# Up-projection in three token blocks with one-bank matmuls, and the weights' Winograd sums kept in DRAM

## The chip, the cores and the metric

One core of one Trainium2 chip. The metric is the device time of one execution in microseconds (us), the median of the runs shown; smaller is better.

## The reference, cut to what matters

One encoder layer in float32 on 2048 + 256 tokens of width 1024: an mLSTM group and a GQA group side by side, then a feed-forward part with a centred depthwise convolution of width 3 over the tokens. The change touches the feed-forward part:

```python
x = x + jnp.concatenate([m_out, a_out], axis=-1) @ w_out
h = rmsnorm(x, norm2_w)
u = centred_dwconv(h @ w_up, conv_w, conv_b)      # w_up: 1024 x 5632
a, g = jnp.split(u, 2, axis=-1)
return x + (jax.nn.silu(g) * a) @ w_down          # w_down: 2816 x 1024
```

Both request groups have the same weights, so the kernel treats the 2304 tokens as one axis and mends the convolution at the seam (token 2048).

## The kernel before, in words

Every product is made of float32r matmuls: an operand is split into a high part (a ScalarE copy) and a low part (a VectorE subtract of the copy from the source), and three matmuls high x high, high x low, low x high are accumulated in PSUM.

The stages follow one another: projections, attention and mLSTM side by side, the output projection with the second RMSNorm (`phase_c`, "C"), the up-projection (`phase_u`, "U") and the down-projection (`phase_e`, "E"). C writes the normalised activations to DRAM (`n2_d`).

**U.** The up-projection is a Winograd product of 2x2 blocks: seven products in place of eight. Tokens go in two blocks of `BLK` = 1152; `DT` gives the columns that each block computes, 1160 and 1144 (a few are shared with the next block's convolution and carried over in `carry`). Each block is cut into two token halves of 580 or 572 columns, and K = 1024 into two halves of four 128-row chunks. For a block, `n2_ops` holds seven activation operands in SBUF ("11", "21", "t2", "t1", "t3", "22", "t4"), each as high and low part of four chunks. The four "t" operands are sums that `n2_sums` makes beforehand on GpSimd (GpSimd DMAs in, four subtracts of 286 or 290 columns a half, DMAs out to `n2t_d`): for block 0 during C, for block 1 during groups 3 to 6 of block 0 (`SG`). `n2_load` reads an operand with two SyncE DMAs, two ScalarE copies and two VectorE subtracts (L1171, L1172).

The weights go in 22 "ups" a block (`up_start`), each for two output chunks of 128 columns, two ups (gate, then value) to a group. An up reads two raw weight tiles (L1206, SyncE, 512 KB each, a ring of two ups); GpSimd makes four weight sums of 512 columns (L1245 to L1248); for each of the seven products ScalarE makes the high part (L1233) and VectorE the low part (L1234), into a ring of five weight tiles (`WU`). `mul` then issues 24 matmuls (L1238): two token quarters of 290 or 286 columns, four chunks, three terms. So an up is 168 matmuls, and U is 44 ups of them. A PSUM tile is two banks, one for each quarter, and four such tiles take turns. ScalarE copies (L1256) and VectorE additions with one input in PSUM (L1259) combine the products to `u`.

The convolution follows for each chunk (`conv`): ScalarE writes the middle tap and the bias (L1341), VectorE adds the two outer taps (`scalar_tensor_tensor`, L1348, four an up). After the value up VectorE multiplies gate and value (L1367, one an up on average). GpSimd makes the four sums that E needs (L1371 to L1376) and stores seven operands to `a_d` (L1357).

**E.** It computes the down-projection in the same way, in seven passes with 384 columns a matmul (L1567). Its operands come by SyncE DMAs (`acts`: tiles `te`, 768 KB; `weight`: tiles `dw`, 256 KB), each split by ScalarE (L1409) and VectorE (L1410).

The order on each engine is written by a scheduler at build time from the program order and from priorities (`high_priority` raises them); on the chip every queue runs in that order. Memory of the pools is a stack: a pool that is opened takes the place of closed ones, and a tile's first write waits for the last reader of what lay there.

Of the kernel before, what the change touches and what calls it, by code (L numbers as in the profile page):

```python
# [17 lines left out]
P = 128  # L18
D = 1024
# [16 lines left out]
BLK = 1152  # L36
# [10 lines left out]
NH = 580  # L47
NW = 2 * NH + 1
DT = (0, 2 * NH, T)
HB = BLK // 2  # L50
TW = T // 2
N2A, N2B = 1280, 1024
# [33 lines left out]
P0 = ((V, V),) * 4  # L86
P1 = ((V, V),) * 7
LOP = ()
DLAG = 6
SEGS = ((0, NT1), (NT1, NT))  # L90


def f32(ap):
    return ap.bitcast(F32)
# [940 lines left out]
def phase_c(g, sn, sp, pp, wps):  # L1035
# [64 lines left out]
    def tail_b(b, x, ps, r):  # L1100
        r = rstd_rows(g, ps, r, BT)
        for z in range(NCC):
            nc.vector.scalar_tensor_tensor(x[:, z], x[:, z], g.n2w[:, z:z + 1], r, ALU.mult, ALU.mult)
            if z % 4 == 3:
                if b * BT < N2A:
                    g.st.dma_start(g.n2_d[0][:, z - 3:z + 1, b * BT:(b + 1) * BT], x[:, z - 3:z + 1])
                if b * BT >= N2B:
                    g.st.dma_start(g.n2_d[1][:, z - 3:z + 1, b * BT - N2B:(b + 1) * BT - N2B], x[:, z - 3:z + 1])
        g.normed.add(b)
# [10 lines left out]
    for n, b in enumerate(order):  # L1120
        x, mx = nxt
        for z in range(4):
            if z == 1 and n + 1 < NB:
                yield 2 * order[n + 1], C_MM
                nxt = loads(n + 1, order[n + 1])
            po = pp.tile([P, 2, BT], F32, tag="po", name=f"po{b}_{z}")
            for k, _ in enumerate(mm(b, z, mx, po)):
                if z == 1 and k == 0 and prev is not None:
                    tail_b(*prev)
                if z < 3 or k < 3:  # L1130
                    yield None, C_MM
            if z == 0:
                if prev is not None:
                    prev = (*prev[0:2], *tail_a(*prev))
                acc = sp.tile([P, 2, BT], F32, tag="acc", name=f"cacc{b}", bufs=1)
            post(b, z, x, po, acc)
            if (n, z) > (5, 0) and sums:

                n2_sums(g, sp, 0, sums.pop(0), tag="rn", bufs=2)
        prev = (b, x, acc)  # L1140
# [8 lines left out]
EARLY, LATE = OPS[:3], OPS[3:]  # L1149
# [7 lines left out]
def n2_load(g, ops, b, k, engs=("vector", "vector")):  # L1157


    nc = g.nc  # L1160
    n = (DT[b + 1] - DT[b]) // 2
    if k[0] == "t":
        i, h = SUMS[k]
        src = g.n2t_d[b, i, :, :, h]
    else:
        t = DT[b] - (0, N2B)[b] + n * (int(k[1]) - 1)
        src = g.n2_d[b][:, NCC // 2 * (int(k[0]) - 1):, t:t + n]
    for z in range(0, NCC // 2, 2):
        hi, lo = (ops[k][:, z:z + 2, a, 0:n] for a in range(2))
        nc.sync.dma_start(f32(lo), src[:, z:z + 2, 0:n])  # L1170
        nc.scalar.activation(hi, f32(lo), AF.Copy)  # L1171
        getattr(nc, engs[z // 2]).tensor_tensor(lo, f32(lo), f32(hi), ALU.subtract)  # L1172
# [6 lines left out]
def n2_sums(g, pool, b, c, engs=("gpsimd",) * 4, tag="tc", bufs=3):  # L1179


    nc = g.nc
    n = (DT[b + 1] - DT[b]) // 2
    m = n // 2
    for z in range(2):
        rs = []
        for k in range(2):
            r = pool.tile([P, NH], F32, tag=tag, name=f"rn{b}_{c}_{z}_{k}", bufs=bufs)[:, 0:n]
            r = r.rearrange("p (h t) -> p h t", h=2)
            src = g.n2_d[b][:, c + NCC // 2 * k, DT[b] - (0, N2B)[b]:DT[b + 1] - (0, N2B)[b]].rearrange("p (h t) -> p h t", h=2)  # L1190
            nc.gpsimd.dma_start(r, src[:, :, z * m:z * m + m])
            rs.append(r)
        (b11, b12), (b21, b22) = ((r[:, 0], r[:, 1]) for r in rs)
        for eng, (o, p, q) in zip(engs, ((b11, b12, b11), (b12, b22, b12), (b22, b22, b11), (b21, b21, b22))):
            getattr(nc, eng).tensor_tensor(o, p, q, ALU.subtract)
        for k in range(2):
            nc.gpsimd.dma_start(g.n2t_d[b, k, :, c, :, z * m:z * m + m], rs[k])
# [17 lines left out]

def up_start(g, s1, bank, ops, b, jj, rs=None):
# [4 lines left out]
    m = n // 2  # L1221
# [6 lines left out]
    def mul(p, k, src, add=False):  # L1228
# [6 lines left out]
        for z in range(2):  # L1235
            for c in range(NCC // 2):
                for i, (aa, bb) in enumerate(((0, 0), (0, 1), (1, 0))):
                    nc.tensor.matmul(p[:, z], w[:, aa, c, :], ops[k][:, c, bb, z * m:z * m + m],  # L1238
                                     start=c == 0 and i == 0 and not add, stop=c == NCC // 2 - 1 and i == 2,
                                     skip_group_check=add)  # L1240
    p1, p2 = bank("a" + nm)[:, :, 0:m], bank("b" + nm)[:, :, 0:m]
# [3 lines left out]
    nc.gpsimd.tensor_tensor(t1, a21, a22, ALU.add)  # L1245
    nc.gpsimd.tensor_tensor(t2, t1, a11, ALU.subtract)
    nc.gpsimd.tensor_tensor(a21, a11, a21, ALU.subtract)
    nc.gpsimd.tensor_tensor(t4, a12, t2, ALU.subtract)  # L1248

    def rest(u1, u2):  # L1250


        u11, u12, u21, u22 = (u[:, k * n:k * n + n].rearrange("p (z t) -> p z t", z=2) for u in (u1, u2) for k in range(2))
# [10 lines left out]
        p3 = bank("c" + nm)[:, :, 0:m]  # L1264
# [14 lines left out]
def phase_u(g, tc, s1, pd, ops, first):  # L1279
# [5 lines left out]
    with ExitStack() as st:  # L1285
        sa = st.enter_context(tc.tile_pool(name="d_a", bufs=1, reuse_waits="tile"))
        for k in range(YB):
            sa.tile([P, BLK], F32, tag="y", name=f"place_y{k}", bufs=YB)
        for k in range(3):
            sa.tile([P, NH], F32, tag="tc", name=f"place_tc{k}", bufs=3)  # L1290
# [18 lines left out]
        late.update(n2_ops(sl2, 0, ("t3", "t1")))  # L1309
        late = {k: late[k] for k in LATE}  # L1310
        for k, e in zip(LATE, P0):
            n2_load(g, late, 0, k, engs=e)
# [3 lines left out]
        def bank(nm):  # L1316
            return banks(g, pd[(g.nbank + 1) // 2 % 2], "p" + nm)
        for b in range(ND):
            nn = DT[b + 1] - DT[b]
            if b:  # L1320
                ops = n2_ops(s1[0], b, EARLY)
                ops.update(n2_ops(sl, b, ("t4", "22")))
                ops.update(n2_ops(sl2, b, ("t3", "t1")))
                for k, e in zip(OPS, P1):
                    n2_load(g, ops, b, k, engs=e)
# [33 lines left out]
            for gi, gr in enumerate(groups):  # L1359
                if b < ND - 1 and SG <= gi < SG + NCC // 2:  # L1360
                    n2_sums(g, sa, b + 1, gi - SG)
                ygs = up(gr[0] + NFC)
# [6 lines left out]
                t1, t2, t4 = (sa.tile([P, NH], F32, tag="tc", name=f"tc{k}_{b}_{gi}", bufs=3)[:, 0:HB] for k in (1, 2, 4))  # L1369
# [11 lines left out]
def phase_e(g, tc, pd):  # L1381
# [5 lines left out]
    with ExitStack() as st:  # L1387
        sx = st.enter_context(tc.tile_pool(name="e_t", bufs=1, reuse_waits="tile"))
        for k in range(TR):
            sx.tile([P, 2, TG, CG], F32R, tag="t", name=f"place_t{k}", bufs=TR)  # L1390
        swa = st.enter_context(tc.tile_pool(name="e_w", bufs=1, reuse_waits="tile"))
        for k in range(WRA):
            swa.tile([P, 2, h], F32R, tag="w", name=f"place_wa{k}", bufs=WRA)
        sr = st.enter_context(tc.tile_pool(name="e_r", bufs=1, reuse_waits="tile"))
        for k in range(DW):
            sr.tile([P, h], F32, tag="dw", name=f"place_dw{k}", bufs=DW)
        sc = st.enter_context(tc.tile_pool(name="e_c", bufs=1, reuse_waits="tile"))
        quad = {k: sc.tile([P, 4, TW], F32, name="c%d%d" % k) for k in ((0, 1), (0, 0), (1, 0), (1, 1))}
        sy = st.enter_context(tc.tile_pool(name="e_x", bufs=1, reuse_waits="tile"))
        for k in range(2):  # L1400
            sy.tile([P, 4, h], F32, tag="x", name=f"place_x{k}", bufs=2)
        sms = {(hf, z): sy.tile([P, CG], F32, tag=f"sm{hf}{z}", name=f"sm{hf}{z}") for hf in range(2) for z in range(G3)}
# [123 lines left out]
        fetch_w(WA)  # L1526
        fetch_t(2)
# [82 lines left out]
def body(tc, aps, phases="abcd"):  # L1610
# [5 lines left out]
    with ExitStack() as st:  # L1616
# [9 lines left out]
        g.n2_d = [dp.tile([P, NCC, n], F32, name=f"n2_d{k}") for k, n in enumerate((N2A, T - N2B))]  # L1626
# [3 lines left out]
        g.a_d = [dp.tile([7, P, min(TG, NP - p), TW], F32, name=f"a_d{p}") for p in range(0, NP, TG)]  # L1630
        g.s_d = [[dp.tile([P, D // 2], F32, name=f"s_d{k}_{p}") for p in range(NP)] for k in range(4)]
# [66 lines left out]
        pd = [pool(s5, "d_u", bufs=1, space=PSUM)]  # L1698
        g.nbank = -1
        with ExitStack() as s2:  # L1700
# [15 lines left out]
            first = [up_start(g, s1, lambda nm: banks(g, pd[(g.nbank + 1) // 2 % 2], "p" + nm), ops, 0, NFC, rs)]  # L1716
            g.c_end()
            s_wo.close()
            pd.append(pool(s5, "d_v", bufs=1, space=PSUM))
            phase_u(g, tc, s1, pd, ops, first)  # L1720
# [94 lines left out]
```

## Time and profile before

| | |
|---|---|
| median of 3 runs | 3371.27 us (3369.89 to 3371.71) |
| the profiled execution | 3363.86 us, its span 3361.9 us |
| mean granted TensorE clock | 0.990 |
| DVE busy | 2399.9 us, 71% |
| ACT busy | 1803.6 us, 54% |
| POOL busy | 1355.2 us, 40% |
| U's matmuls | from 1806.8 us to 2836.5 us |
| E's matmuls | from 2843.6 us on |

PE is TensorE, DVE VectorE, ACT ScalarE, POOL GpSimd, SP SyncE. In a table of windows each engine's busy time stands beside the number of instructions in brackets, then the granted clock, the share of time that the 16 DMA engines were busy, and GB/s. In a list of groups a line gives the source line, the engine, the operation, the tiles written and read, the shape and the count, then the busy time and the mean ns of one, then idle time before it. In a view of one source line, "a/b/c" are the least, the median and the longest duration in ns. In a list of waits a line names who waited, for whom, how long in total, how often, and the longest.

### The profile page before, as it was taken

The numbers are of one execution on the slowest core, as the hardware profiler recorded it, in microseconds if no ns is written. First come the engines' busy times: TensorE is split into PE (matmuls) and PEld (weight loads), VectorE is DVE, ScalarE is ACT, GpSimd is POOL, SyncE is SP. The second block draws the span as 40 slices with busy tenths as digits, with TensorE's granted clock in tenths as the row PEclk, the third lists the DMA queues.
The fourth block names the chain that finished last, engine by engine and source line by source line (L and its number), as shares of the span: only waits on it lengthen the run. The fifth ranks groups of instructions, "written<-read, shape, count | busy, mean of one in ns | idle before, by whom it ended". The sixth has DMA issues, their size and how long they took to land. (4 is left out here: it accounts for less than half of the span.)

```text
span 3361.9 us, 57158 instructions
## 1 busy us (share of the span) xinstructions
PE 3262.6 (97%) x21366; PEld 3038.9 (90%) x21366; DVE 2399.9 (71%) x3721; ACT 1803.6 (54%) x3799; POOL 1355.2 (40%) x1710
## 2 busy tenths in 40 slices
PE   8899999999999999899999999999999999999998
PEld 6788888888888888788888999999999998999998
DVE  7866687777768778976765778978877776453573
ACT  5546666667666777655553544446555555323331
POOL 8653033213333323421245457744544442751112
PEclk9999999999999999999999999999999999999999
DMA  8665333343336444433347334424232223875563
GB/s 273 224 202 165 94 118 106 99 129 94 118 105 190 131 134 127 124 111 96 99 141 262 116 109 141 146 88 177 100 100 94 94 100 110 303 259 173 174 217 105
DMA packets 300636, 483.03 MB, mean 144 GB/s; under 512 B 36597, under 2 KB 186279, under 8 KB 300359
## 3 DMA queue, kind: packets, MB, share of 16 engines
q1 hardware_dynamic: 247543, 348.34, 32.7%
q0 software_dynamic: 36256, 121.60, 10.9%
q10 hardware_dynamic: 16560, 9.44, 0.9%
q8 instruction: 168, 2.75, 0.3%
q14 instruction: 109, 0.89, 0.1%
HBM read 337.37 MB, written 141.91 MB: 143 GB/s over the span
## 5 line engine op out<-in xcount | busy, mean ns | idle before, releaser
L634 DVE TENSOR_TENSOR pl<-ps,ph 128x512 fp32r<-128x512 f32 x520 | 353.9, 684 | 206.8 <-ACT ps L633 194.8
L1238 PE MATMUL pa<-nt,wut 128*128 128x290 f32 (+1 forms) x3168 | 447.0, 297 | 7.8 <-ACT u L1256 5.7
L632 ACT ACTIVATE ph<-ps 128x512 fp32r<-128x512 f32 x520 | 309.8, 596 | 248.7 <-PE ps L629 243.3
L1238 PEld LDWEIGHTS pa<-nt,wut 128*128 128x128 f32 x3168 | 431.1, 189 | 10.3 <-ACT u L1256 7.8
L603 DVE TENSOR_REDUCE mx<-px 128x1 f32<-128x512 f32 (+1 forms) x528 | 346.3, 673 | 94.3 <-PE px L602 92.2
L1348 DVE SCALAR_TENSOR_TENSOR y<-u,cw,y 128x1152 f32<-128x1152 f32 (+1 forms) x176 | 319.1, 1813 | 38.3 <-ACT yc L1346 17.3
L646 PE MATMUL pv<-ph,v 128*128 128x512 f32 (+1 forms) x1040 | 318.8, 401 | 0.8 <-ACT ph L632 0.3
L633 ACT ACTIVATE ps<-ps 128x512 f32<-128x512 f32 x520 | 310.2, 597 | 0.0
L1567 PE MATMUL et<-tet,wet 128*128 128x384 f32 x1584 | 279.0, 336 | 0.0
L1567 PEld LDWEIGHTS et<-tet,wet 128*128 128x128 f32 x1584 | 277.1, 188 | 0.0
L1081 PEld LDWEIGHTS po<-cmx,wo 128*128 128x128 f32 x1728 | 222.3, 192 | 9.7 <-DVE cmx L1069 1.5
L1081 PE MATMUL po<-cmx,wo 128*128 128x256 f32 x1728 | 226.4, 285 | 1.5 <-DVE cmx L1069 1.3
L1567 PE MATMUL e<-te,we 128*128 128x384 f32 x1188 | 213.5, 340 | 13.1 <-ACT te L1409 7.1
L1567 PEld LDWEIGHTS e<-te,we 128*128 128x128 f32 x1188 | 210.7, 190 | 14.5 <-ACT te L1409 7.3
L628 PE MATMUL ps<-qq,kk 128*128 128x512 f32 x520 | 214.9, 415 | 4.6 <-DVE mx L603 2.8
L602 PE MATMUL px<-kk,qq 128*128 128x512 f32 (+1 forms) x528 | 203.0, 412 | 4.1 <-DVE mx L603 2.4
L629 PE MATMUL ps<-qm,kl 65*128 65x512 f32 x520 | 205.9, 398 | 0.0
L792 PE MATMUL mj<-mn,wm 128*128 128x256 f32 x1296 | 197.9, 287 | 5.4 <-ACT og L808 3.4
L792 PEld LDWEIGHTS mj<-mn,wm 128*128 128x128 f32 x1296 | 182.7, 191 | 21.6 <-ACT og L808 3.8
L802 PEld LDWEIGHTS mv<-wm,mn 128*128 128x128 f32 x1296 | 183.1, 190 | 18.0 <-ACT qb L798 1.9
L802 PE MATMUL mv<-wm,mn 128*128 128x256 f32 x1296 | 196.9, 285 | 1.2 <-ACT qb L798 1.1
L646 PE MATMUL pv<-pl,v 128*128 128x512 f32 x520 | 191.6, 400 | 0.1
(310 smaller groups left out, 7244.9 us busy)
## 6 DMA issues: line engine op xcount, KB each, us to landing
mn<-n_d SPq DMA_DIRECT2D x216, 256.0 KB, 3.2
ru<-w_up SPq DMA_DIRECT2D x88, 512.0 KB, 3.6
a_d<-y POOLq DMA_DIRECT2D x88, 288.0 KB, 2.6
a_d<-tc POOLq DMA_DIRECT2D x66, 288.0 KB, 2.9
n_d<-n1T SPq DMA_DIRECT2D x18, 1024.0 KB, 5.3
dm<-nm_d POOLq DMA_DIRECT2D x72, 256.0 KB, 4.1
mjn<-n_d SPq DMA_DIRECT2D x72, 256.0 KB, 3.6
mvn<-n_d SPq DMA_DIRECT2D x72, 256.0 KB, 3.1
```

The source lines that it names most:

```text
L603: nc.vector.tensor_reduce(s.mx[:, t, z0:z0 + 1], ps[:, 0:w], AX.X, ALU.max)
L628: nc.tensor.matmul(ps, kk[:, kc:kc + P], s.qq[:, 0:N], start=True, stop=False)
L632: nc.scalar.activation(ph, ps, AF.Exp)
L633: nc.scalar.activation(ps, ps, AF.Exp)
L634: nc.vector.tensor_tensor(pl, ps, f32(ph), ALU.subtract)
L646: nc.tensor.matmul(s.pv[0:HD if k in (1, 3) else P, 0:N], v, p, start=(kp == 0 and k == 0), stop=(2 * kp + 2 == s.nk and k == 5))
L792: nc.tensor.matmul(pj[:, o], s.w[c][:, a, o * P:(o + 1) * P], nT[c][:, :, h, :], start=(c + o + k == 0), stop=(c == NCC - 1 and k == 2 and ...
L802: nc.tensor.matmul(pv[:, o], nT[c][:, o, a, :], s.w[c][:, h, 256:512], start=(c + o + k == 0), stop=(c == NCC - 1 and k == 2 and o == 1))
L1081: nc.tensor.matmul(po[:, o], wo[z // 2][c][:, a, n], mx[c][:, h, :], start=(c == 0 and k == 0), stop=(c == NCC - 1 and k == 2))
L1238: nc.tensor.matmul(p[:, z], w[:, aa, c, :], ops[k][:, c, bb, z * m:z * m + m], start=c == 0 and i == 0 and not add, stop=c == NCC // 2 - 1 ...
L1348: nc.vector.scalar_tensor_tensor(y[:, s:e], u[:, s + k:e + k], cw[:, k, jj:jj + 1], y[:, s:e], ALU.mult, ALU.add)
L1567: nc.tensor.matmul(ps[m // 2][:, m % 2], w[:, aa, m * P:(m + 1) * P], t[:, bb], start=p == 0 and n == 0, stop=p == NP - 1 and n == 2)
```

## The change

U goes in three blocks of 768 tokens (`DT` = 0, 772, 1540, 2304: halves of 386, 384 and 382 columns), so a product is 12 matmuls of 386 columns in one PSUM bank, and eight banks take turns singly (`bank1`). The three weight sums that are products' inputs and the fourth, `a21`, are still made on GpSimd in block 0, which now also writes them to DRAM (`u_d`) by SyncE; blocks 1 and 2 read them from there, 256 KB each, in place of the GpSimd work and of half a raw tile. Four of the seven operands ("11", "21", "t2", "t1") get a second set of buffers and are read for the next block during groups 7 to 10; three are read at the start of a block. `n2_sums` works on a whole half at once, and for block 0 it starts one token block of C earlier. E's pools are stacked in another order, so that its `te` tiles lie where block 1's operands were and its first weight tiles under block 2's "11" and "21", and its first two `te` tiles and first two weight tiles are fetched with a raised priority.

```diff
-BLK = 1152
+BLK = 768
-NH = 580
+NH = 386
-DT = (0, 2 * NH, T)
+DT = (0, 2 * NH, 4 * NH - 4, T)
-N2A, N2B = 1280, 1024
+N2R = ((0, 1024), (768, 1792), (1536, T))
...
-            if (n, z) > (5, 0) and sums:
+            if (n, z) > (4, 0) and sums:
...
-EARLY, LATE = OPS[:3], OPS[3:]
+EARLY, LATE = OPS[:4], OPS[4:]
...
+def n2_sums(g, pool, b, c):
     nc = g.nc
     n = (DT[b + 1] - DT[b]) // 2
+    rs = []
+    for k in range(2):
+        r = pool.tile([P, 2, NH], F32, tag="rn", name=f"rn{b}_{c}_{k}", bufs=2)[:, :, 0:n]
+        t = DT[b] - N2R[b][0]
+        nc.gpsimd.dma_start(r, g.n2_d[b][:, c + NCC // 2 * k, t:t + 2 * n].rearrange("p (h t) -> p h t", h=2))
+        rs.append(r)
+    (b11, b12), (b21, b22) = ((r[:, 0], r[:, 1]) for r in rs)
+    for o, p, q in ((b11, b12, b11), (b12, b22, b12), (b22, b22, b11), (b21, b21, b22)):
+        nc.gpsimd.tensor_tensor(o, p, q, ALU.subtract)
+    for k in range(2):
+        nc.gpsimd.dma_start(g.n2t_d[b, k, :, c, :, 0:n], rs[k])
...
     for k, r in enumerate(rs):
-        g.nc.sync.dma_start(r, g.w_up[jj + k].rearrange("p c n -> p (c n)"))
+        if b and k:
+            g.nc.sync.dma_start(r[:, 0:D // 2], g.u_d[jj // 2][3])
+            g.nc.sync.dma_start(r[:, D // 2:D], g.w_up[jj + k, :, NCC // 2:].rearrange("p c n -> p (c n)"))
+        else:
+            g.nc.sync.dma_start(r, g.w_up[jj + k].rearrange("p c n -> p (c n)"))
...
+def bank1(g, pools, name):
+    k = g.nbank = g.nbank + 1
+    return pools[k // 4 % 2].tile([P, 512], F32, tag=f"q{k % 4}", name=name, bufs=1)
...
-        for z in range(2):
-            for c in range(NCC // 2):
-                for i, (aa, bb) in enumerate(((0, 0), (0, 1), (1, 0))):
-                    nc.tensor.matmul(p[:, z], w[:, aa, c, :], ops[k][:, c, bb, z * m:z * m + m],
+        for c in range(NCC // 2):
+            for i, (aa, bb) in enumerate(((0, 0), (0, 1), (1, 0))):
+                nc.tensor.matmul(p, w[:, aa, c, :], ops[k][:, c, bb, 0:n],
...
-    nc.gpsimd.tensor_tensor(t1, a21, a22, ALU.add)
-    nc.gpsimd.tensor_tensor(t2, t1, a11, ALU.subtract)
-    nc.gpsimd.tensor_tensor(a21, a11, a21, ALU.subtract)
-    nc.gpsimd.tensor_tensor(t4, a12, t2, ALU.subtract)
+    ts = list(enumerate((t2, t1, t4, a21)))
+    if b:
+        for k, t in ts[:3]:
+            nc.sync.dma_start(t, g.u_d[jj // 2][k])
+    else:
+        nc.gpsimd.tensor_tensor(t1, a21, a22, ALU.add)
+        nc.gpsimd.tensor_tensor(t2, t1, a11, ALU.subtract)
+        nc.gpsimd.tensor_tensor(a21, a11, a21, ALU.subtract)
+        nc.gpsimd.tensor_tensor(t4, a12, t2, ALU.subtract)
+        for k, t in ts:
+            nc.sync.dma_start(g.u_d[jj // 2][k], t)
...
+        sb = st.enter_context(tc.tile_pool(name="d_b", bufs=1, reuse_waits="tile"))
+        n2_ops(sb, "place", EARLY)
...
             if b:
-                ops = n2_ops(s1[0], b, EARLY)
+                ops = nxt
                 ops.update(n2_ops(sl, b, ("t4", "22")))
-                ops.update(n2_ops(sl2, b, ("t3", "t1")))
-                for k, e in zip(OPS, P1):
-                    n2_load(g, ops, b, k, engs=e)
+                ops.update(n2_ops(sl2, b, ("t3",)))
+                for k in LATE:
+                    n2_load(g, ops, b, k)
...
+                if b < ND - 1 and gi == SG + NCC // 2:
+                    nxt = n2_ops(s1[0] if b % 2 else sb, b + 1, EARLY)
+                if b < ND - 1 and 0 <= gi - SG - NCC // 2 < len(EARLY):
+                    n2_load(g, nxt, b + 1, EARLY[gi - SG - NCC // 2])
...
-        fetch_w(WA)
-        fetch_t(2)
+        with tc.high_priority(offset=MPRI):
+            fetch_t(1)
+            fetch_w(WA)
+            fetch_t(1)
```

More of the change, by code (lines that the diff above doesn't have):

```diff
@@ L1171, in n2_load @@
         nc.scalar.activation(hi, f32(lo), AF.Copy)
-        getattr(nc, engs[z // 2]).tensor_tensor(lo, f32(lo), f32(hi), ALU.subtract)
+        nc.vector.tensor_tensor(lo, f32(lo), f32(hi), ALU.subtract)
 SUMS = {"t1": (0, 0), "t3": (0, 1), "t4": (1, 0), "t2": (1, 1)}
-def n2_sums(g, pool, b, c, engs=("gpsimd",) * 4, tag="tc", bufs=3):
+def n2_sums(g, pool, b, c):
     nc = g.nc
     n = (DT[b + 1] - DT[b]) // 2
-    m = n // 2
-    for z in range(2):
[L1186 to L1197, printed above, removed]
+    rs = []
[9 more added lines that the diff above has]
+        nc.gpsimd.dma_start(g.n2t_d[b, k, :, c, :, 0:n], rs[k])
 def up_load(g, pools, b, jj):
@@ L1276, with phase_u @@
 DOPS = ("11", "21", "t4", "t2", "t3", "t1", "22")
-def phase_u(g, tc, s1, pd, ops, first):
+def phase_u(g, tc, s1, pu, ops, first):
     nc = g.nc
@@ L1289, in phase_u @@
         for k in range(3):
-            sa.tile([P, NH], F32, tag="tc", name=f"place_tc{k}", bufs=3)
+            sa.tile([P, HB], F32, tag="tc", name=f"place_tc{k}", bufs=3)
+        for k in range(2):
+            sa.tile([P, 2, NH], F32, tag="rn", name=f"place_rn{k}", bufs=2)
         sp = st.enter_context(tc.tile_pool(name="d_s", bufs=2, reuse_waits="tile"))
@@ L1308, in phase_u @@
         sl2 = st.enter_context(tc.tile_pool(name="d_r", bufs=1, reuse_waits="tile"))
[L1309 to L1312, printed above, removed]
+        late.update(n2_ops(sl2, 0, ("t3",)))
+        for k in LATE:
+            n2_load(g, late, 0, k)
         ops.update(late)
@@ L1387, in phase_e @@
     with ExitStack() as st:
+        sr = st.enter_context(tc.tile_pool(name="e_r", bufs=1, reuse_waits="tile"))
+        for k in range(DW):
+            sr.tile([P, h], F32, tag="dw", name=f"place_dw{k}", bufs=DW)
+        swa = st.enter_context(tc.tile_pool(name="e_w", bufs=1, reuse_waits="tile"))
+        for k in range(WRA):
+            swa.tile([P, 2, h], F32R, tag="w", name=f"place_wa{k}", bufs=WRA)
+        sc = st.enter_context(tc.tile_pool(name="e_c", bufs=1, reuse_waits="tile"))
+        quad = {k: sc.tile([P, 4, TW], F32, name="c%d%d" % k) for k in ((0, 1), (0, 0))}
+        hz = [(hf, z) for hf in range(2) for z in range(G3)]
+        sms = {k: sc.tile([P, CG], F32, name="sm%d%d" % k) for k in hz[:4]}
+        sc.tile([P, EGAP], F32, name="e_gap")
         sx = st.enter_context(tc.tile_pool(name="e_t", bufs=1, reuse_waits="tile"))
@@ L1625, in body @@
         dram("n1_d", [NB, P, NCC, 2, 2, P])
-        g.n2_d = [dp.tile([P, NCC, n], F32, name=f"n2_d{k}") for k, n in enumerate((N2A, T - N2B))]
+        g.n2_d = [dp.tile([P, NCC, hi - lo], F32, name=f"n2_d{k}") for k, (lo, hi) in enumerate(N2R)]
         dram("n2t_d", [len(DT) - 1, 2, P, NCC // 2, 2, NH])
@@ L1630, in body @@
         g.a_d = [dp.tile([7, P, min(TG, NP - p), TW], F32, name=f"a_d{p}") for p in range(0, NP, TG)]
+        g.u_d = [[dp.tile([P, D // 2], F32, name=f"u_d{p}_{k}") for k in range(4)] for p in range(NFC)]
         g.s_d = [[dp.tile([P, D // 2], F32, name=f"s_d{k}_{p}") for p in range(NP)] for k in range(4)]
@@ L1697, in body @@
         s5 = st.enter_context(ExitStack())
-        pd = [pool(s5, "d_u", bufs=1, space=PSUM)]
+        s6 = s5.enter_context(ExitStack())
+        pu = [pool(s6, "d_u", bufs=1, space=PSUM)]
         g.nbank = -1
@@ L1714, in body @@
                 f()
-            first = [up_start(g, s1, lambda nm: banks(g, pd[(g.nbank + 1) // 2 % 2], "p" + nm), ops, 0, NFC, rs)]
+            first = [up_start(g, s1, lambda nm: bank1(g, pu, "p" + nm), ops, 0, NFC, rs)]
             g.c_end()
             s_wo.close()
-            pd.append(pool(s5, "d_v", bufs=1, space=PSUM))
-            phase_u(g, tc, s1, pd, ops, first)
+            pu.append(pool(s6, "d_v", bufs=1, space=PSUM))
+            phase_u(g, tc, s1, pu, ops, first)
+        s6.close()
+        pd = [pool(s5, f"d_e{k}", bufs=1, space=PSUM) for k in range(2)]
+        g.nbank = 2
         phase_e(g, tc, pd)
```

45 lines of the change are left out of this document (18 added, 27 removed).

## The prediction

> **What bounds the kernel now.** I read the page first, then the table of windows over U and E, then the waits of TensorE at the seams, then the groups of VectorE and GpSimd inside U. The page says that TensorE is nearly always busy:
>
> ```profile
> PE 3262.6 (97%) x21366; PEld 3038.9 (90%) x21366; DVE 2399.9 (71%) x3721; ACT 1803.6 (54%) x3799; POOL 1355.2 (40%) x1710
> ```
>
> So a change in U can gain in two ways only: fewer nanoseconds for the same columns, or fewer gaps at the seams. It can lose wherever another engine stops keeping up. The windows (block 0 twice, block 1 twice, E) carry the pace:
>
> ```profile
> 2060.00:2160.00 100.00, 99.95 (x742) 99.54 (x741) 87.77 (x67) 45.88 (x71) 78.28 (x77) 1.00 0.47 150
> 2160.00:2260.00 100.00, 100.00 (x746) 100.00 (x745) 81.10 (x66) 46.55 (x70) 55.49 (x49) 1.00 0.27 94
> 2500.00:2600.00 100.00, 100.00 (x757) 100.00 (x756) 74.42 (x68) 55.96 (x102) 46.53 (x44) 1.00 0.27 93
> 2600.00:2700.00 100.00, 100.00 (x757) 100.00 (x756) 69.68 (x67) 52.82 (x97) 44.77 (x41) 1.00 0.28 95
> 3000.00:3100.00 100.00, 100.00 (x574) 100.00 (x573) 43.16 (x35) 36.91 (x37) 20.25 (x17) 1.00 0.61 195
> ```
>
> The count beside PE gives the pitch: 100 us / 746 = 134.0 ns with 290 columns, 100 / 757 = 132.1 ns with 286, 100 / 574 = 174.2 ns with E's 384. The second thing to see is VectorE's column: 70% in block 1, but 81 to 88% in block 0, for the same instructions an up. TensorE lost nothing by it, yet the margin was small.
>
> The seams are the other place. TensorE's waits at the start of U, between the two blocks, and at the start of E, three views in this order:
>
> ```profile
> PE pa L1238 <- ACT nt L1171: 2.0, 1, 2.0
> PE pc L1238 <- ACT u L1256: 1.6, 1, 1.6
> PE pc L1238 <- ACT wut L1233: 1.3, 1, 1.3
> ...
> PE pa L1238 <- ACT u L1256: 2.4, 2, 2.3
> PE pa L1238 <- DVE wu L1234: 0.6, 1, 0.6
> PE pc L1238 <- DVE wut L1234: 0.3, 1, 0.3
> PE pc L1238 <- DVE nt L1172: 0.3, 1, 0.3
> ...
> PE e L1567 <- ACT te L1409: 7.1, 1, 7.1
> PE e L1567 <- DVE we L1410: 5.2, 1, 5.2
> PE e L1567 <- DVE te L1410: 0.8, 1, 0.8
> ```
>
> That is 4.9 us, 3.6 us and 13.1 us.
>
> **The matmuls.** From 286 to 384 columns the pitch grows by (174.2 - 132.1) / 98 = 0.430 ns a column, so 386 columns take 175.1 ns and 382 take 173.3. The columns in all stay the same; 1848 matmuls fewer pay their fixed part. Before: 22 x 168 = 3696 matmuls a block, 3696 x (134.0 + 132.1) ns = 983.5 us. After: 22 x 84 = 1848 a block, 1848 x (175.1 + 174.2 + 173.3) ns = 965.8 us. Gain 17.7 us, good to about 2 (one matmul more or less in a window).
>
> **VectorE and GpSimd in block 0.** An up now lasts 84 x 175.1 ns = 14.71 us in place of 22.5, but its weights still take seven subtracts on VectorE and, in block 0, four sums on GpSimd, and these do not shrink. Their lone cost is the median (or, for GpSimd's sums in blocks and VectorE's large ones, the value from which most of them don't stray), here with least/median/longest in ns:
>
> ```profile
> L1234 DVE TENSOR_TENSOR wut<-ru,wut x84: 672/686/3326, 1889.3 to 2822.0; 128x512 fp32r<-128x512 f32 x84
> L1259 DVE TENSOR_TENSOR u<-pa,u x43: 745/755/765, 1880.4 to 2830.3; 128x572 f32<-128x572 f32 x22, 128x580 f32<-128x580 f32 x21
> L1348 DVE SCALAR_TENSOR_TENSOR y<-u,cw,y x169: 1402/1419/4362, 1886.2 to 2835.8; 128x1152 f32<-128x1152 f32 x85, 128x1151 f32<-128x1151 f32 x84
> L1367 DVE TENSOR_TENSOR y<-y,y x42: 1343/1358/2455, 1889.9 to 2804.2; 128x1152 f32<-128x1152 f32 x42
> L1172 DVE TENSOR_TENSOR nt<-nt x8: 1335/1339/2445, 2338.3 to 2363.5; 128x1144 fp32r<-128x1144 f32 x8
> L1195 POOL TENSOR_TENSOR rn<-rn x16: 682/704/1418, 2002.5 to 2167.9; 128x286 f32<-128x286 f32 x16
> L1245 POOL TENSOR_TENSOR tw<-ru x41: 1277/1294/2275, 1882.0 to 2787.2; 128x512 f32<-128x512 f32 x41
> L1371 POOL TENSOR_TENSOR tc<-y x21: 1430/1441/2259, 1892.2 to 2797.5; 128x576 f32<-128x576 f32 x21
> ```
>
> The longest tell why VectorE was slower in block 0. A stretch of the timeline shows it:
>
> ```profile
> 2499.83 0.75 DVE L1259 TENSOR_TENSOR u<-pc,u 128x572 f32<-128x572 f32 x1 [1.76 <-PE pc L1238]
> 2499.93 1.29 POOL L1245 TENSOR_TENSOR tw<-ru 128x512 f32<-128x512 f32 x1
> 2500.50 1.29 DVE L1234 TENSOR_TENSOR wut<-tw,wut 128x512 fp32r<-128x512 f32 x1
> 2502.24 3.82 DVE L1348 SCALAR_TENSOR_TENSOR y<-u,cw,y 128x1152 f32<-128x1152 f32 x1 [0.46 <-ACT yc L1346]
> 2502.28 1.30 POOL L1246 TENSOR_TENSOR tw<-tw,ru 128x512 f32<-128x512 f32 x1
> 2503.54 1.30 POOL L1247 TENSOR_TENSOR ru<-ru,ru 128x512 f32<-128x512 f32 x1
> ```
>
> The addition with one input in PSUM takes its 0.75 us beside a GpSimd sum, and its longest in the row above is 0.765. The subtract with both inputs in SBUF begins at 2500.50 and ends 0.57 us after the GpSimd sum has (2501.22): it waited. The tap at 2502.24 waits for two sums in a row and lasts 3.82 us in place of 1.42. So a two-input VectorE instruction and a GpSimd sum take turns.
>
> VectorE an up before, alone: 7 x 0.69 + 3 x 0.755 + 4 x 1.419 + 1.358 = 14.13 us; GpSimd's sums: 4 x 1.295 + 2 x 1.44 = 8.06 us, and in groups 3 to 6 of block 0 eight subtracts of 0.70 a group, 2.8 us an up. In the window from 2060 there are 742 / 168 = 4.417 ups: VectorE alone would be 62.4 us, it was busy 87.8, so 25.4 us of waiting against 4.417 x 10.86 = 48.0 us of GpSimd's sums, a share of 0.53. In the window from 2600: 4.506 ups, 63.7 alone, 69.7 busy, 6.0 against 36.3, a share of 0.17. These are the two ends.
>
> After, with 1.044 ns a column between 512 and 1152 columns on VectorE: taps 1.02, product 0.96, addition 0.56, an operand's subtract of 772 columns 0.95. An up: 4.83 + 1.67 + 4.07 + 0.96 = 11.53 us. GpSimd (2.68 ns a column from 286 to 512): 4 x 1.295 + 2 x 0.95 = 7.08 us. Groups 3 to 6 add four subtracts of 0.96 on GpSimd, 1.92 an up; groups 7 to 10 add two operand subtracts on VectorE, 0.95 an up. With a share s of GpSimd's time on VectorE's path, block 0 takes 6 x (11.53 + 7.08 s) + 8 x (11.53 + 9.00 s) + 8 x (12.48 + 7.08 s) = 261.2 + 171.1 s us of VectorE, against 22 x 14.71 = 323.6 of TensorE. Five weight tiles stand ready ahead of TensorE, 5 x 12 x 0.175 = 10.5 us that are spent once. So nothing is lost up to s = 0.43, and every 0.01 above costs 1.7 us. With 0.17 the cost is 0, with 0.53 it is 17.8 us. The nearest row is the one from 2060, the same block and the fullest VectorE; VectorE will be fuller still, so I take s = 0.56: 357.0 - 323.6 - 10.5 = +23 us. A gain is excluded, since TensorE's pitch is counted above.
>
> In blocks 1 and 2 the weight sums are gone from GpSimd, 1.9 us an up remains (3.8 in block 1's groups 3 to 6): 11.53 + 0.53 x 3.8 = 13.5 us at most beside 14.6. No cost; without that cover, at s = 1, 0.7 us in each of eight ups.
>
> **Transfers and queues.** Blocks 1 and 2 read 1792 KB an up in place of 1024 and store 672: 2464 KB in 14.6 us, 170 GB/s, against 93 GB/s at a DMA share of 0.27 in the window from 2500; by proportion a share of 0.5, below E's 0.61 beside a full TensorE. Block 0 writes 1024 KB more: 2720 KB, 0.55. The queue of SyncE is where it could hurt: a store of a weight sum waits there for GpSimd, and behind it stand the raw weights of later ups, and in groups 7 to 10 the operands. The raw weights have a ring of two ups, 29 us, against this landing:
>
> ```profile
> ru<-w_up SPq DMA_DIRECT2D x88, 512.0 KB, 3.6
> ```
>
> I cost it at nothing; if the cover fails, 1 us an up in 44 ups is 44 us (a rival below). ScalarE was busy 56 us in 4.5 ups, 12.4 an up: even if nothing of that shrank it would fit in 14.6.
>
> **The seams.** Between blocks only three operands are read late in place of seven, but twice: 3.6 x 3/7 x 2 = 3.1 us, a gain of 0.5; from 0 to twice 3.6 us. At U's start the sums begin a block of C earlier, and t1 is among the early operands: the 2.0 us for `nt` go, the other two waits belong to weights and copies and stay: gain 2, from 0 to 4.9.
>
> At E's start the first `te` tile is read and split long before U ends, so 7.1 + 0.8 us go. The 5.2 us come from later weights, on a busy DMA; two `te` loads fewer stand there, while VectorE must still do U's last convolution first, so I take half, 2.6. There is a third part, in the windows of that place:
>
> ```profile
> 2845.50:2867.00 21.50, 21.50 (x113) 21.20 (x114) 13.49 (x14) 8.93 (x14) 12.11 (x17) 0.92 0.73 254
> 2867.00:2872.60 5.60, 0.38 (x3) 0.06 (x2) 5.60 (x3) 1.48 (x3) 5.58 (x6) 0.71 0.51 205
> 2872.60:2900.00 27.40, 27.40 (x148) 27.40 (x149) 9.98 (x6) 6.22 (x6) 19.43 (x25) 0.94 0.87 303
> ```
>
> After each gap the granted clock is 0.92 and 0.94: 113 matmuls in 21.5 us and 148 in 27.4, where 174.2 ns each make 19.7 and 25.8. Of these 3.4 us I take 2.5. Gain 13, from 3 to 16.5.
>
> **The sum.** -17.7 + 23 - 0.5 - 2 - 13 = -10 us. The profiled execution was 3363.9 us, 2 outside its span; it lies 7.4 below the median of 3371.3. I take the difference from the median: 3361. For this kernel 0.2%, 6.7 us, is about what a measurement can tell from no change.
>
> **The rivals.**
> Slower: GpSimd and VectorE take turns more strictly in block 0. It decides from s = 0.62, where the cost is 33 and eats all gains. For it: from 70 to 88% of VectorE's time the share rose from 0.17 to 0.53, and at 100% each sum that starts finds an instruction waiting. Against it: the two fit beside a full TensorE from 2060 to 2160. At s = 0.70 block 0 loses 57.4 - 10.5 = 47, the sum is +14, 3385. The Trainium skill, "SBUF — State Buffer", section "Who interferes with whom", says that a VectorE instruction with two SBUF inputs and a GpSimd instruction that reads SBUF hold one lock for the whole instruction; the timeline above agrees. By that rule with full durations an up would need 9.86 + 7.08 = 16.9 us, 18.9 in groups 3 to 6 and 17.9 in groups 7 to 10, 395.6 in all, and the sum would be +28, about 3400.
>
> Faster by far: the scheduler interleaves the two so that s stays under 0.43, as in block 1. Then block 0 costs nothing: -33, 3338. Against it: what kept s at 0.17 was VectorE's idle third.
>
> No difference: E's start keeps 10 of its 13 us, since U's last convolution delays the third weight tile. -10 + 10 = 0, 3371.
>
> Slower by the queue: the sums from DRAM come late in blocks 1 and 2, +44: 3405. For it only that three tiles hold one up's sums; against it the loads' 3.6 us.
>
> **How the numbers follow.** Forecast 0.32, stricter turns 0.25, cover holds 0.18, E's start 0.18, queue 0.07. Of the forecast 0.27 is faster by over 0.2% and 0.05 is within; of E's start 0.02 and 0.15, with 0.01 slower; of the stricter turns 0.02 within and 0.23 slower. So faster 0.27 + 0.18 + 0.02 = 0.47, same 0.05 + 0.15 + 0.02 = 0.22, slower 0.01 + 0.23 + 0.07 = 0.31. The range reaches from the cover that holds, 3338, nearly to the strict lock, 3396. The forecast's own range, s from 0.53 to 0.60, is 3356 to 3368.
>
> **What would show it.** Right: 386-column windows with about 571 matmuls per 100 us in blocks 1 and 2; in block 0 VectorE over 95% busy and TensorE waiting for weight tiles (L1234's successor), some 23 us in all; E's first wait gone. Wrong: block 0 at full pace with VectorE under 90%; or blocks 1 and 2 with TensorE waiting on loads of the stored sums; or E's first passes still at a lowered clock.

## The result, and the profile after

The changed kernel is slower: 3421.22 us median of 4 runs (3415.48 to 3427.86) against 3370.58 (3361.95 to 3371.71) for the kernel before, a ratio of 1.0157 with a 95% interval of 1.0131 to 1.0182. The profiled execution has a span of 3413.8 us, 51.9 us more. First the page, then the windows that answer to those of before (one each of blocks 0, 1 and 2 and of E), then TensorE's waits in block 0 and at E's start:

```profile
PE 3265.3 (96%) x19518; PEld 3027.5 (89%) x19518; DVE 2539.7 (74%) x4065; ACT 1918.0 (56%) x4209; POOL 1268.6 (37%) x1711
```

```profile
1900.00:2200.00 300.00, 255.11 (x1325) 246.54 (x1324) 270.51 (x241) 139.70 (x257) 200.14 (x193) 0.94 0.53 177
2300.00:2400.00 100.00, 99.71 (x567) 99.07 (x566) 82.50 (x102) 60.31 (x123) 31.79 (x43) 1.00 0.55 179
2600.00:2700.00 100.00, 95.43 (x542) 94.47 (x542) 78.27 (x97) 65.47 (x144) 26.32 (x36) 1.00 0.52 162
3000.00:3100.00 100.00, 100.00 (x575) 99.73 (x574) 54.62 (x36) 31.34 (x33) 64.92 (x72) 1.00 0.79 264
```

```profile
PE pa L1241 <- ACT u L1266: 22.7, 12, 4.4
PE pc L1241 <- ACT u L1266: 19.1, 7, 6.1
PE pa L1241 <- DVE wu L1238: 7.0, 3, 3.9
...
PE e L1591 <- DVE te L1432: 1.1, 1, 1.1
PE e L1591 <- ACT we L1431: 1.1, 1, 1.1
```

Block 0 made 1325 matmuls in 300 us, 226 ns each, at a granted clock of 0.94; block 1 made 567 in 100 us, 176 ns, with TensorE full. TensorE's page line hides this (97% to 96%): a matmul counts as busy for 193 ns in the first of these windows (255.11 us / 1325) and for 176 ns in block 1's, and block 0 is one eighth of the span.

Where the 51.9 us are, from the ends of the stages in the two timelines (before; after):

```profile
1826.68 5.85 PE L1081 MATMUL po<-cmx,wo 128*128 128x256 f32 x48
2833.18 3.34 PE L1238 MATMUL pa<-nt,wut 128*128 128x286 f32 x24
```

```profile
1810.32 11.55 PE L1080 MATMUL po<-cmx,wo 128*128 128x256 f32 x96
...
2904.42 2.26 PE L1241 MATMUL pa<-nt,wut 128*128 128x382 f32 x12
2907.77 22.42 PE L1591 MATMUL e<-te,we 128*128 128x384 f32 x127 [1.10 <-ACT we L1431]
```

| | before | after | difference |
|---|---|---|---|
| C's last matmuls end | 1832.5 | 1821.9 | -10.6 |
| from there to U's last matmul | 1004.0 | 1084.8 | +80.8 |
| from there to E's first | 7.1 | 1.1 | -6.0 |
| from there to the end | 518.3 | 506.0 | -12.3 |

So the seams gained 28.9 us and U lost 80.8. After the change, block 1's first matmul starts at 2233.2 and block 2's at 2560.6: block 0 took 411 us, block 1 327 (177 ns for each of its 1848 matmuls), block 2 346. At block 1's pace throughout, U would have taken 3 x 327.4 = 982 us, 22 less than before. Block 0 lost 84 us against that pace, block 2 18. A stretch of block 0's timeline shows what happens there:

```profile
1919.73 0.88 POOL L1190 TENSOR_TENSOR rn<-rn 128x384 f32<-128x384 f32 x1
1920.17 3.76 DVE L1362 SCALAR_TENSOR_TENSOR y<-u,cw,y 128x767 f32<-128x767 f32 x1
1920.55 1.30 POOL L1254 TENSOR_TENSOR tw<-tw,ru 128x512 f32<-128x512 f32 x1
1921.81 1.29 POOL L1255 TENSOR_TENSOR ru<-ru,ru 128x512 f32<-128x512 f32 x1
...
1923.85 3.85 DVE L1238 TENSOR_TENSOR wut<-ru,wut 128x512 fp32r<-128x512 f32 x1
1924.35 1.00 POOL L1394 TENSOR_TENSOR tc<-y,tc 128x384 f32<-128x384 f32 x1
1925.29 0.56 POOL L1371 DMA_DIRECT2D a_d<-y  x1
1925.86 1.27 POOL L1256 TENSOR_TENSOR tw<-ru,tw 128x512 f32<-128x512 f32 x1
...
1928.66 0.84 ACT L1382 ACTIVATE y<-y 128x768 f32<-128x768 f32 x1 [8.35 <-DVE y L1362]
1929.41 0.47 ACT L1266 ACTIVATE u<-pc 128x386 f32<-128x386 f32 x1
...
1929.94 0.69 PE L1241 MATMUL pc<-n,wu 128*128 128x386 f32 x1 [6.09 <-ACT u L1266]
```

VectorE's tap, 1.0 us alone, lasts 3.76 us beside three GpSimd sums in a row, and its subtract, 0.69 alone, 3.85 beside the next two (GpSimd's DMA issues between them are in part left out above). Silu waits for the taps, the PSUM copies stand behind Silu in ScalarE's queue, and TensorE waits 6.09 us for a copy.

### The profile page after: what moved, and what is told of

It reads as the page before. It is cut to its first block, busy times and chain, and to the rows that moved or that the text cites. A ratio compares the mean times of both kernels' runs of the same rounds, so it can differ in the third digit from the quotient of the medians.

```text
span 3413.8 us, 55270 instructions
## 1 busy us (share of the span) xinstructions
PE 3265.3 (96%) x19518; PEld 3027.5 (89%) x19518; DVE 2539.7 (74%) x4065; ACT 1918.0 (56%) x4209; POOL 1268.6 (37%) x1711
## 3 DMA queue, kind: packets, MB, share of 16 engines
q0 software_dynamic: 38464, 121.61, 10.6%
## 5 line engine op out<-in xcount | busy, mean ns | idle before, releaser
L1241 PE MATMUL pa<-nt,wut 128*128 128x386 f32 (+2 forms) x2376 | 458.4, 343 | 32.4 <-ACT u L1266 28.1
L1362 DVE SCALAR_TENSOR_TENSOR y<-u,cw,y 128x768 f32<-128x768 f32 (+1 forms) x264 | 325.6, 1234 | 27.1 <-ACT y L1355 16.2
L1371 POOL DMA_DIRECT2D a_d<-y x132 | 73.6, 558 | 429.2 <-DVE y L1385 429.2
```

What stands on the lines that cost most here:

```text
L1241: nc.tensor.matmul(p, w[:, aa, c, :], ops[k][:, c, bb, 0:n], start=c == 0 and i == 0 and not add, stop=c == NCC // 2 - 1 and i == 2, skip_ ...
L1362: nc.vector.scalar_tensor_tensor(y[:, s:e], u[:, s + k:e + k], cw[:, k, jj:jj + 1], y[:, s:e], ALU.mult, ALU.add)
```

## The experiments

The theory after the result, theory 1: in block 0 GpSimd's sums and VectorE's two-input instructions shut each other out, and an up of 14.9 us (84 x 177 ns) has no room for both. Rivals: the stores of the sums on SyncE's queue (2), and VectorE's own work without GpSimd (3). The row under an experiment is its window from 1900 to 2200, to be read against the first window row above. Where block 0 is faster, this window reaches into block 1: by 19 us without sums, 32 with memsets, 5 with the sums on VectorE. So the time of block 0 as a whole, from C's last matmul to block 1's first, is given too (411 us in the changed kernel). The kernel before was measured beside each on the same chip, with medians from 3365.3 to 3368.3; the ratio is to it.

**No sums, no stores.**

```diff
-        nc.gpsimd.tensor_tensor(t1, a21, a22, ALU.add)    # and the other three, and their stores
+    for k, t in ts[:3]:
+        nc.sync.dma_start(t, half(k))                     # a half of w_up, in every block
```

> Leaves out the four weight sums on GpSimd and their stores; every block reads plain halves of w_up by DMA where it would read the sums, so the products are of other weights, with the same instructions on TensorE, VectorE and ScalarE. Theory 1 (GpSimd's sums and VectorE's two-input instructions shut each other out in block 0) and theory 2 (the stores of the sums hold SyncE's queue and the tiles): block 0 falls from some 411 us to 325 to 340, the total to about 3340. Theory 3 (VectorE's own work is too much for an up of 14.8 us, whatever GpSimd does): block 0 stays over 390 us, the total over 3400.

Measured 3357.26, ratio 0.9974 (0.9965 to 0.9984).

```profile
1900.00:2200.00 300.00, 287.92 (x1591) 285.86 (x1590) 250.06 (x300) 174.07 (x318) 107.39 (x135) 0.98 0.61 202
```

Theory 3 falls as far as it speaks of VectorE without the sums. The gain is 64 us in place of 81: block 0 falls to 351 us, not to 325 to 340, and stays 24 over block 1's 327. What makes these 24 is not shown.

**No stores.**

```diff
-        for k, t in ts:
-            nc.sync.dma_start(g.u_d[jj // 2][k], t)
```

> Keeps the four GpSimd sums in block 0 but leaves out their stores to DRAM; blocks 1 and 2 read plain halves of w_up in their place, as many bytes. Theory 1: no more than 10 us faster than the changed kernel, 3410 to 3421. Theory 2: block 0 recovers, 3345 to 3360. Theory 3: 3410 to 3421.

Measured 3439.1, 1.022 (1.0205 to 1.0236).

```profile
1900.00:2200.00 300.00, 252.71 (x1294) 246.61 (x1294) 262.83 (x234) 133.97 (x247) 195.58 (x188) 0.91 0.36 120
```

Theory 2 falls: with a third less DMA block 0 is no faster (424 us). Theory 1 had 3410 to 3421, so this is 18 us more than any theory said. In the profile block 0 has 13 us more than in the changed kernel, and E 7. The scheduler wrote another order here (U's first matmul comes at C's end, in the changed kernel 12 us before it); whether that is the reason is not shown.

**GpSimd busy, but not reading.**

```diff
-        nc.gpsimd.tensor_tensor(t1, a21, a22, ALU.add)    # and the other three
+        for t in (t1, t2, a21, t4):
+            for _ in range(2):
+                nc.gpsimd.memset(t, 0.0)
```

> In block 0 each GpSimd sum is replaced by two GpSimd memsets of the same tile, about 1.1 us of GpSimd in place of 1.3, which write SBUF but read none of it; the stores stay, the products are of zeros. Theory 1, if it is GpSimd's reading that shuts VectorE out: VectorE's subtracts keep their 0.69 us beside them, block 0 falls to 330 to 350 us, the total to 3340 to 3360. Theory 1 with a lock on writes too, theory 2 and theory 3: 3400 or more.

Measured 3350.89, 0.9961 (0.9946 to 0.9975). Its window and the larger group of memsets in it; then VectorE's subtracts in that window (least, median and longest ns; two of four groups); then the same two groups of the changed kernel:

```profile
1900.00:2200.00 300.00, 293.63 (x1651) 291.30 (x1650) 263.12 (x310) 180.73 (x332) 182.74 (x281) 1.00 0.68 232
L1255 POOL MEMSET tw<- 128x512 f32 x100 | 52.1, 535 | 28.8 <-DVE wut L1238 15.2 <-DVE wu L1238 8.4 <-DMA u_d<-tw 4.6
```

```profile
L1238 DVE TENSOR_TENSOR wut<-ru,wut x40: 675/686/2145, 1899.7 to 2199.9; 128x512 fp32r<-128x512 f32 x40
L1238 DVE TENSOR_TENSOR wu<-tw,wu x20: 677/686/1926, 1910.7 to 2195.8; 128x512 fp32r<-128x512 f32 x20
```

```profile
L1238 DVE TENSOR_TENSOR wut<-ru,wut x32: 676/1492/3850, 1901.1 to 2193.0; 128x512 fp32r<-128x512 f32 x32
L1238 DVE TENSOR_TENSOR wu<-tw,wu x15: 676/1483/3328, 1918.1 to 2190.7; 128x512 fp32r<-128x512 f32 x15
```

This is the run that decides. Block 0 takes 337 us, with the stores in place and TensorE at a clock of 1.00. GpSimd is busy for 183 of 300 us, against 200. Of these 183 the memsets are 69 (17.0 of them on the raw tile), where the sums took 102 us in the changed kernel, part of it waiting; the rest is what both kernels have: E's sums, the operands' sums, the issuing of DMAs. All four groups of subtracts now have a median of 0.69 us. In the changed kernel the other two groups had that median too, with some of up to 3.99 us; the mean of all subtracts falls from 1.23 to 0.89. What slows VectorE is that GpSimd's sums read SBUF, not that GpSimd is busy. This fits the Trainium skill, "SBUF — State Buffer", section "Who interferes with whom", which speaks of GpSimd instructions that read and excepts those that only write.

**The sums on VectorE.**

```diff
-        nc.gpsimd.tensor_tensor(t1, a21, a22, ALU.add)    # and the other three
+        nc.vector.tensor_tensor(t1, a21, a22, ALU.add)
```

> The four sums of block 0 are made on VectorE in place of GpSimd, nothing left out. Theory 1: VectorE's own work rises by 4 x 0.69 = 2.8 us to 14.3 us an up, but GpSimd's 5.2 us are gone; with 0.5 of the remaining GpSimd time on its path 15.2 to 16.2 us an up, block 0 about 350, the total 3355 to 3370. Theory 2: no change, 3421. Theory 3: slower than the changed kernel, over 3440.

Measured 3381.93, 1.0041 (1.0026 to 1.0055).

```profile
1900.00:2200.00 300.00, 282.25 (x1549) 277.42 (x1549) 280.30 (x353) 168.26 (x308) 108.56 (x135) 0.98 0.59 208
```

VectorE does more and block 0 is faster, 194 ns a matmul in this window where the changed kernel took 226; the whole is 39 us shorter than the changed kernel. VectorE takes 280.3 us for 1549 / 84 = 18.4 ups, 15.2 us each, the low end of what was worked out, and is busy 93% of the time. The total is 12 us over the expectation, because block 0 took 367 us in place of about 350: as in the changed kernel, an up (16.3 us) takes longer than VectorE is busy with it.

**Split taps** in block 2, for its waits:

```diff
-                if cut < BLK:                 # small ScalarE instructions: two columns saved,
-                    nc.scalar.activation(...) # and mended after the taps
+                    c = cut - k // 2
+                    for s, e in ((s, e),) if cut >= BLK else ((s, c), (c + 1, e)):
+                        nc.vector.scalar_tensor_tensor(y[:, s:e], ...)
```

> The changed kernel with the seam at token 2048 (it lies in block 2) mended in another way: VectorE's two outer taps skip one column each there, in two pieces, and the six small ScalarE instructions a chunk that mended it are gone; nothing is left out. Theory S (block 2's 16 us of TensorE waits on weight tiles come from ScalarE, which waits at the mend for VectorE's taps with the next weights' high parts queued behind it): block 2's waits fall under 4 us, the total by 10 to 14 us, to about 3408. Rival (VectorE's own load in block 2): VectorE gets 0.7 us an up more, the waits stay or grow, the total 3420 to 3430.

Measured 3411.38, 1.013 (1.011 to 1.0151), 10 us less. (The mend was three ScalarE instructions a chunk, six an up.) TensorE's longest waits in block 2, the changed kernel and this one; last, ScalarE's wait at the mend in the changed kernel:

```profile
PE pa L1241 <- DVE wu L1238: 6.4, 5, 1.6
PE pb L1241 <- DVE wu L1238: 4.6, 3, 1.5
PE pa L1241 <- ACT u L1266: 4.5, 4, 2.8
```

```profile
PE pa L1241 <- ACT u L1266: 1.5, 2, 1.2
PE pc L1241 <- DVE wut L1238: 1.4, 1, 1.4
```

```profile
ACT y L1366 <- DVE y L1362: 40.1, 20, 3.3
```

Theory S holds: VectorE has more to do in block 2, its rival, and yet block 2 falls from 346 to 332 us and TensorE's waits there from 18 to 6 us. The kernel before had the same mend in its block 1, with 22 us an up to hide it.

**Longer rows**, for the matmul's pitch, which came out at 176 ns for 384 columns where the prediction had 174.2: tiles of 400 elements a row for two operands. The edit also makes the empty tile in front of E's operand tiles, `e_gap`, 304 elements long in place of 80.

> The changed kernel with rows of 400 in place of 386 elements in two of the seven operands (11 and 21) of blocks 0 and 2; the columns that matmuls read stay. Theory P (a row of 1544 bytes makes the 386- and 384-column matmuls of U 1.6 ns longer than E's): the products of these two operands take 1.5 to 2 ns a matmul less than the others of their block. Rival (something else in U): no difference between the products. The total stays at 3415 to 3430 in both.

A single run, 3434.79. In block 2's timeline a product with long rows (`pb`) and one with short rows (`pc<-nt`) follow each other:

```profile
2654.88 2.25 PE L1241 MATMUL pb<-n,wu 128*128 128x382 f32 x12
2656.97 2.25 PE L1241 MATMUL pc<-nt,wut 128*128 128x382 f32 x12
2659.05 2.27 PE L1241 MATMUL pa<-nt,wut 128*128 128x382 f32 x12
```

2.09 and 2.08 us from start to start: theory P falls, and the 2 ns stay unexplained. In the same run E's own pitch rose: 568 matmuls from 3000 to 3100 us in place of 575, both with TensorE full and the clock at 1.00. E's tiles lie elsewhere there, by the longer `e_gap`. Whether the place of the tiles is also what parts U's pitch from E's was not tested.

**Both mends at once**, sums on VectorE and split taps.

> Both at once, nothing left out: block 0's sums on VectorE, and the seam mended by split taps. If block 0's and block 2's losses are separate, the gains add up: 3382 less 10 to 14, 3368 to 3372, no different from the kernel before. If they are not, 3380.

Measured 3370.96, 1.0005 (0.9988 to 1.0022): the two add up, and the kernel is level with the one before, not better.

**E's fetch without the raised priority**, `fetch_w(WA)` and `fetch_t(2)` as before, pools in their new places.

> The changed kernel with E's first operand and weight tiles fetched in the old way, two weight tiles and then two operand tiles, without the raised priority; the new places of the pools stay. Theory E1 (the early fetch is what took the 13 us of waits at E's start away): 8 to 13 us slower than the changed kernel, with waits of 7 us before E's first matmul. Rival (the new places alone do it, since the buffers come free earlier): within 3 us of 3421.

Measured 3423.76, 1.0167 (1.0145 to 1.0188), and E begins as early:

```profile
PE e L1589 <- DVE te L1432: 1.6, 1, 1.6
PE e L1589 <- ACT we L1431: 1.1, 1, 1.1
```

The raised priority made none of the gain at E's start. That the places of the buffers made it, the rival, fits, but they do not do it alone, as **E's part alone** below shows.

**No Silu**, to see whether the queue of ScalarE is the limit.

```diff
-                for y in ygs:
-                    nc.scalar.activation(y, y, AF.Silu)
```

> The changed kernel without the Silu on the gate's tiles (left out: the product is gate times value without it), GpSimd's sums as they are. Theory C (a chain through the order of ScalarE's queue: GpSimd holds VectorE's tap up, Silu waits for the tap, and the PSUM copy for which TensorE waits stands behind Silu): TensorE's waits for u (40 of 58 us in block 0) fall under 15, the total by 25 to 40 us, to 3380 to 3396, with VectorE over 93% busy in block 0. Rival (VectorE's time together with GpSimd's is the limit by itself, whatever ScalarE does): the waits move to the weight tiles, the total stays within 8 us of 3421.

Measured 3415.47, 1.014 (1.0124 to 1.0157). Window, and TensorE's waits in block 0:

```profile
1900.00:2200.00 300.00, 254.14 (x1330) 243.43 (x1329) 275.06 (x240) 127.28 (x240) 206.09 (x198) 0.95 0.53 179
```

```profile
PE pa L1241 <- DVE wut L1238: 17.2, 4, 6.9
PE pa L1241 <- ACT u L1266: 13.5, 11, 3.3
PE pc L1241 <- ACT u L1266: 10.0, 4, 5.1
PE pa L1241 <- DVE wu L1238: 9.5, 5, 2.8
```

Theory C falls: of the 42 us of waits for copies 24 remain, those for weight tiles grow from 12 to 30, and the pace stays (block 0 416 us). The chain in the timeline above is how the lateness reaches TensorE, not where it comes from.

**Two sums on each engine**, with split taps: `t1` and `t2` by `nc.vector`, the other two by `nc.gpsimd`.

> Split taps, and of block 0's four sums t1 and t2 are made on VectorE, the other two on GpSimd; nothing is left out. A dose between the kernel with all four on GpSimd (3411 with split taps) and that with all four on VectorE (3371). Theory 1 (every GpSimd instruction that reads SBUF costs VectorE's path the same share, 0.65 as measured): 12.9 + 0.65 x 4.5 = 15.8 us an up against 14.3 + 0.65 x 1.9 = 15.5: 3375 to 3385. Rival (it is the handing back and forth that costs, so that half the sums cost as much as all): over 3400.

Measured 3383.7, 1.0049 (1.0032 to 1.0065).

```profile
1900.00:2200.00 300.00, 274.32 (x1461) 267.62 (x1462) 277.68 (x302) 153.10 (x282) 157.38 (x167) 0.95 0.56 194
```

3411, 3384 and 3371 for four, two and no sums on GpSimd, as theory 1 had it: the first two sums that leave GpSimd bring 28 us, the other two 13.

**E's part alone**, on the kernel before: raw and first weight tiles at the bottom, operand tiles above them, raised priority.

> The kernel before (two blocks) with only E's part of the change: the raw and first weight tiles of E lie at the bottom, under the operands 11 and 21, the operand tiles above them, and the first ones are fetched with raised priority; nothing is left out. Theory E2 (the waits at E's start, 13 us, come from where the tiles lie and need no third block): 8 to 14 us faster than the kernel before, with the first wait under 2 us. Rival (without the free second set of operand buffers the first operand tile comes as late as ever): within 4 us of the kernel before.

Measured 3367.48 against 3368.26, 0.9994 (0.9984 to 1.0004): no difference.

```profile
PE e L1569 <- ACT we L1409: 6.7, 2, 4.8
PE e L1569 <- DVE we L1410: 2.5, 2, 1.7
```

The waits shrink from 13.1 to 9.5 us only. So the early operand tiles seem to need the operand buffers that the third block leaves free; no run frees these alone.

**t4 in place**, to loosen the ring of small weight tiles.

```diff
+    t4 = s1[0].tile([P, h], F32, tag="tmp", ...) if b else a12
```

> The changed kernel, nothing left out; in block 0 the sum t4 is written over its own source (the second half of the first raw tile, split long before) in place of a third small tile, so that t1 of an up no longer waits until t1 of the up before has been split. Theory R (part of block 0's loss beyond the taking of turns is this ring: GpSimd waited 36 us for VectorE's splits between 1900 and 2200 us, and VectorE then for GpSimd): GpSimd's waits fall under 10 us, block 0 and the total by 20 us or more, under 3402. Rival (VectorE's and GpSimd's joint time is the limit, GpSimd only starts earlier): GpSimd's waits fall, the total stays within 8 us of 3421.

Measured 3424.9, 1.0173 (1.015 to 1.0196). GpSimd's waits from 1900 to 2200 us, the changed kernel and this one:

```profile
POOL tw L1253 <- DVE wut L1238: 35.8, 11, 8.6
```

```profile
POOL tw L1254 <- DMA ru<-w_up: 31.2, 8, 8.0
POOL tw L1254 <- DVE wut L1239: 9.7, 2, 5.0
```

The wait did not go but moved: the raw tile is now held longer, and GpSimd waits for the next load. Block 0 takes 415 us. So the run does not tell whether GpSimd's waits cost anything.

## Why the prediction was wrong

The forecast was -10 us, the result +51 of the median. The sign was that of its first rival, stricter turns in block 0, which it had at +14 and, by the rule with full durations, at +28.

*"So I take s = 0.56: 357.0 - 323.6 - 10.5 = +23 us"* is the step that failed: it let block 0 last as long as VectorE's instructions with their waiting turns, as if VectorE never stood still, and took a lead off. Block 0 lost 84 us. The share was not far off: from 1900 to 2200 there are 1325 / 84 = 15.8 ups, VectorE alone 11.53 x 15.8 = 182 and some 3 for operands, busy 270.5, so 86 us of waiting against 15.8 x 7.08 + 21 x 0.95 = 132 us of GpSimd, 0.65. In the formula that makes 38 us, 15 more than 0.56. The other 46 are time in which VectorE stood still. VectorE is busy 270.5 / 15.8 = 17.1 us with an up, but an up took 19.0: a tenth of the time it waited, 16 of 300 us for TensorE's products and 12 for ScalarE's copies. Its longest waits in that window:

```profile
DVE u L1269 <- PE pc L1241: 8.8, 5, 2.7
DVE u L1269 <- PE pa L1241: 7.3, 4, 3.5
```

TensorE and ScalarE waited for VectorE in their turn, and GpSimd for its tiles. The lead of five weight tiles, 10.5 us, was not seen as a gain anywhere. The prediction's own sign was VectorE over 95% busy and TensorE waiting for weight tiles; VectorE was busy 90%, and TensorE waited mostly for copies (42 us of 55). From 1900 to 2200 the clock was 0.94, and a matmul counts as busy for 193 ns in place of 176. That the reading of GpSimd's sums is the cause of block 0's loss is shown (memsets, no sums, the dose). How the 46 us divide between engines that wait for each other is not: of the two runs that took on one link each, Silu left the pace as it was, and the ring's wait only moved.

The stretch of timeline at 2499.83 that the prediction gives for block 0 of the old kernel lies in its block 1, which began at 2341.6. It shows the same instructions taking turns, so the reading stands.

The matmuls: predicted -17.7, from pitches of 175.1, 174.2 and 173.3 ns. Block 1's 384 columns took 176 ns in place of 174.2 (in E, of the same run, 575 in 100 us, 173.9). With 1.8 ns more on 5544 matmuls the gain is 8 us. The pitch read in E did not carry over to U.

Blocks 1 and 2: "No cost" was right for block 1 (567 a window, VectorE at 82%). Block 2 cost 18 us, put at nothing. The working had VectorE's and ScalarE's busy time, which fits, and left out the order: the mend of the seam, in block 2 alone, makes ScalarE wait for VectorE (40.1 us in block 2) with weights behind it.

Transfers: right. A DMA share of 0.55 was forecast for block 0 and 0.5 after it, 0.53 and 0.55 were measured, and without the stores block 0 was no faster.

The seams: right in sign, too small. At E's start 13 were forecast, 18 came (6.0 before the first matmul, 12.3 after it, with the clock at full). At U's start 2 were forecast and C ended 10.6 us earlier: from 1750 to 1800 us TensorE now made 400 matmuls at a clock of 1.00, before 335 at 0.94. In the old kernel TensorE had waited there for steps of C's RMSNorm on GpSimd (4.6 us in one place). That the earlier sums freed GpSimd for them is likely, and not tested. Between the blocks nothing stands out.

## What to carry to other kernels

Work that a tile costs once, whatever its width, grows against the matmuls when the tile gets narrower: here seven subtracts and four sums went from 22.5 us of cover to 14.7. Add up what takes turns, not what each engine does alone, and treat that as a lower bound: here engines in fixed order, each waiting for the other, took 19.0 us an up where VectorE with its waiting turns was busy 17.1. A sum that moves from GpSimd to VectorE can make VectorE's work longer and its path shorter.

## What the runs showed of the hardware

GpSimd memsets of 512 columns, 69 us of them in a 300 us window, left VectorE's subtract at a median of 0.69 us, where GpSimd sums of the same size, 102 us with their waits, made two of its four groups 1.48 and 1.49. An addition with one input in PSUM kept its 0.54 to 0.56 us beside the same sums.

In the changed kernel VectorE did not get in between GpSimd instructions that followed closely: the subtract at 1923.85 waited through two sums with a DMA issue of 0.56 us between them and ended 0.57 us after the second. The issue alone does not seem to hold it: in the run with memsets a subtract at 2005.66 waited for one sum (2005.46 to 2006.63) and ended 0.54 us after it, while a DMA issue that had begun at 2006.56 was still running. Why the first subtract waited through both sums is open.

E's pitch, with the same matmuls of 384 columns, was 575 to 577 matmuls from 3000 to 3100 us in ten profiles, of the changed kernel and of nine that were made from it, and 568 in that of the longer rows, where `e_gap` moved E's tiles. The granted clock was 1.00 in all of these (the run without stores had 0.98 there, with gaps, and is not counted).
